# First mixer of a diffusion trunk: scores from plain rows of two heads side by side plus rotary rows in four row groups

## The chip, the cores and the metric

The kernel runs on one NeuronCore of a Trainium2 chip, in one launch. The metric is the time of an execution in device microseconds; several executions give a median. The core has five engines that work beside each other, each in its own program order: TensorE (PE in the profile; its weight loads are PEld), VectorE (DVE), ScalarE (ACT), GpSimd (POOL) and SyncE (SP). Here POOL and SP issue DMAs, and ACT issues a few.

## The reference, cut to what matters

Two groups of tokens, 256 latent and 128 context ones, go through a trunk of two layers. Each layer is a half-step SwiGLU FFN, a mixer and another half-step FFN, all modulated by vectors that come from `SiLU(cond) @ w_mod`. The mixer of layer 0 is multi-head latent attention beside a convolution module:

```
cq, ckv, kr, u = split(h @ w_in, [384, 640, 672])
q = (rms_norm(cq) @ w_qu).reshape(B, S, 8, 64 + 32)       # 64 plain columns, 32 rotary ones, per head
q = concat([q[..., :64], axial_rope(q[..., 64:])])        # latent tokens only
k = concat([k_nope, broadcast(axial_rope(kr))])           # 64 rows of the head, 32 shared by all heads
p = softmax(q @ k.T * 96 ** -0.5); o = p @ v
g = depthwise_conv(a * sigmoid(b), w_dw, 31 taps)         # 512 channels
g = silu(layer_norm(g))
out = concat([o, g]) @ w_out
```

Latent queries read the 128 cached context keys and the 256 latent keys; context queries read the 128 context keys.

## The kernel before, in words

All activations are held turned, channels on the 128 partitions and the 384 tokens (256 latent, then 128 context) along the row. Large products are made of three fp32r products (`mm3`): weights and activations are split into a high part (`hi`, a cast on ACT) and a low part (`lo`, the rest), and `hi*hi + hi*lo + lo*hi` is added up in PSUM. `stream` walks through a list of `Step`s; each has a block of weights that SP loads to `raw`, that is split (`split_hi`, `split_lo`) and that its `mm` then uses. With `add=True` the low part is not made by DVE: ACT writes `-raw` to `lo` and a DMA issued by POOL adds `raw` minus the rounding onto it; in the trace that is an ACTIVATE of L176 and a DMA of L177.

The tile framework decides the order of the instructions on each engine when the kernel is built, from the program order and its own priorities; on the chip each engine follows that order strictly and waits on semaphores.

The first mixer, `mixer_a`, goes through these stages:

1. Seven input units (`in_unit`) of `w_in_a`, in the order `ORD`. Their results start the convolution: for each of four channel blocks 31 taps on DVE (`acc<-ub,vec,acc`, L926 and L929), 124 in all. The taps are put in a background list, and `pop_bg` hands out 9 after each step and after each pair of heads.
2. `p_kr` turns the shared rotary key `krf` and copies its 32 rows (held four times over the 128 partitions) to the upper or lower half of all eight `kT` tiles (L890). A `kT` tile of a head then has 64 plain rows and 64 rows with the rotary part twice.
3. `q_step(0)`, `kv_step`, `q_step(1)`. A query step makes four heads of 128 columns: 64 plain ones, 32 rotary ones and the same 32 with swapped neighbours. DVE multiplies the PSUM result by a table of 1, cos and sin (`ropeaq`, L940); as the key has its rotary rows twice, the product with 128 rows gives the rotated score. `kv_step` makes keys and values, and calls `first`: scores and softmax of the first pair of heads.
4. `rest`: for each of the four pairs, scores of the next pair (`scores`, L674), then transposes, `p @ v` and the softmax of the next pair. A pair's scores fill four PSUM banks of the pool `ps_mm`, which has four. `softmax` takes maxima on DVE (`mx`, L689) and exponentials on ACT (L694). What a pair gives is `t<-ps_ax,g` on DVE (L731), and then split to `MXh`, `MXl`.
5. After the last tap, `conv_ln`: `centre` (PE, L1009, needs all four `acc`), squares, `scale`, `finish`, which gives blocks 4 to 7 of `MXh`, `MXl`.
6. The output projection. The first halves of three steps (72 products, blocks 0 to 3) can run before `conv_ln` is done; the rest (120 products) begins with block 4, and then the next FFN follows.

The second mixer, `mixer_c`, uses the same `attention` with 64-row heads, two of them side by side in the two halves of the array (`pairs`).

## Time and profile before

| | us |
|---|---|
| median of three executions | 1458.6 (1457.44 to 1465.83) |
| the profiled execution's own time | 1458.97 |
| its span, first to last instruction | 1457.1 |
| PE busy in the span | 1429.5 (98%) |
| DVE busy | 1154.0 (79%) |
| ACT busy | 667.9 (46%) |
| first mixer, from its first product to the first product of the next FFN | 302 to 464 on the trace's clock |

The profile gives times of one execution in us from the span's start. In a timeline row the first number is the start, the second how long it lasted, then the engine, the line, the operation and `out<-in`, how many instructions were merged (x), and in square brackets how long the engine had been idle and what ended that. The f32 products of L674 are two instructions each in the trace. Matmuls are pipelined, so that a row of PE lasts longer than the distance to the next start; the distance is what a product costs.

### The profile page before, as it was taken

The page shows a single profiled execution, that of the slowest core. Times are in us where ns is not written, and L with a number is a line of the kernel's source. Part 1 is how long each engine was busy: PE and PEld are TensorE (multiplying, and loading weights), DVE is VectorE, ACT ScalarE, POOL GpSimd, SP SyncE. Part 2 cuts the span into 40 slices and gives each one's busy share as a digit, 9 for nine tenths or more (in the row PEclk, how much of TensorE's full clock was granted, in tenths as well). Part 3 has the DMA queues.
Part 4 walks back from the last instruction along what each step waited for, and adds up shares of the span by engine and source line. Part 5 has one row for each costly group of instructions (what it writes and reads, how often), then busy time and mean ns, then how long its engine had stood idle before and what let it go on. Part 6 is the DMA issues. An engine that isn't in the chain of part 4 may idle for free. (4 is left out here: it accounts for less than half of the span.)

```text
span 1457.1 us, 22136 instructions
## 1 busy us (share of the span) xinstructions
PE 1429.5 (98%) x8450; PEld 1389.4 (95%) x8450; DVE 1154.0 (79%) x2411; ACT 667.9 (46%) x1177; POOL 26.2 (2%) x38
## 2 busy tenths in 40 slices
PE   8999999999999999999999999999998999999997
PEld 6999999999888999999999999999976999999997
DVE  5899999959987999999879996545887698555443
ACT  4534333368766443343343433334477444434332
POOL 0000000021100000000000000000000000000000
PEclk9999999999999999999999999999999999999999
DMA  9666657699656566556565662344310264332341
GB/s 382 253 226 211 234 187 257 238 245 212 150 145 217 188 228 234 206 213 238 199 243 205 232 229 98 104 136 163 130 59 30 86 230 147 137 124 90 118 135 48
DMA packets 45066, 262.55 MB, mean 180 GB/s; under 512 B 4992, under 2 KB 6816, under 8 KB 22048
## 3 DMA queue, kind: packets, MB, share of 16 engines
q1 hardware_dynamic: 38592, 245.04, 46.8%
q0 software_dynamic: 4032, 14.16, 5.2%
q10 hardware_dynamic: 2336, 1.94, 0.4%
q8 instruction: 67, 1.10, 0.3%
q14 instruction: 39, 0.32, 0.1%
HBM read 244.98 MB, written 1.98 MB: 169 GB/s over the span
## 5 line engine op out<-in xcount | busy, mean ns | idle before, releaser
L167 ACT CAST whi<-raw 128x1024 fp32r<-128x1024 f32 (+1 forms) x346 | 328.0, 948 | 569.3 <-PE ps_mm L271 499.0
L269 PE MATMUL ps_mm<-Hh,wlo 128*128 128x386 f32 x1568 | 531.8, 339 | 1.0 <-DMA wlo<-raw 1.0
L270 PE MATMUL ps_mm<-Hl,whi 128*128 128x386 f32 x1568 | 529.8, 338 | 0.0
L271 PE MATMUL ps_mm<-Hh,whi 128*128 128x386 f32 x1568 | 529.3, 338 | 0.0
L179 DVE TENSOR_TENSOR wlo<-raw,whi 128x1024 fp32r<-128x1024 f32 (+2 forms) x318 | 345.8, 1087 | 149.4 <-ACT whi L167 147.3
L269 PEld LDWEIGHTS ps_mm<-Hh,wlo 128*128 128x128 f32 x1568 | 296.2, 189 | 3.2 <-PE ps_mm L271 1.3
L270 PEld LDWEIGHTS ps_mm<-Hl,whi 128*128 128x128 f32 x1568 | 296.3, 189 | 0.5
L271 PEld LDWEIGHTS ps_mm<-Hh,whi 128*128 128x128 f32 x1568 | 296.6, 189 | 0.0
L269 PE MATMUL ps_mm<-Gh,wlo 128*128 128x384 f32 x704 | 236.5, 336 | 0.0
L270 PE MATMUL ps_mm<-Gl,whi 128*128 128x384 f32 x704 | 236.5, 336 | 0.0
L271 PE MATMUL ps_mm<-Gh,whi 128*128 128x384 f32 x704 | 236.5, 336 | 0.0
L387 DVE SCALAR_TENSOR_TENSOR junk<-rawm,eb 128x1024 bf16<-128x1024 f32 x128 | 155.7, 1217 | 1.1 <-ACT eb L148 1.1
L387 DVE SCALAR_TENSOR_TENSOR rawm<-rawm,eb 128x1024 f32<-128x1024 f32 x128 | 155.7, 1216 | 0.3
L269 PEld LDWEIGHTS ps_mm<-Gh,wlo 128*128 128x128 f32 x704 | 132.4, 188 | 0.0
L270 PEld LDWEIGHTS ps_mm<-Gl,whi 128*128 128x128 f32 x704 | 132.4, 188 | 0.0
L271 PEld LDWEIGHTS ps_mm<-Gh,whi 128*128 128x128 f32 x704 | 132.3, 188 | 0.0
L640 ACT CAST Gh<-g 128x384 fp32r<-128x384 f32 x88 | 45.0, 512 | 89.9 <-DVE g L556 89.7
L549 ACT ACTIVATE sa<-ta,ba 128x256 f32<-128x256 f32 (+1 forms) x176 | 70.3, 447 | 4.4 <-DVE ta L546 4.2
L929 DVE SCALAR_TENSOR_TENSOR acc<-ub,vec,acc 128x399 f32<-128x399 f32 x120 | 69.8, 627 | 0.3
L556 DVE SCALAR_TENSOR_TENSOR g<-t,bb,sa 128x256 f32<-128x256 f32 (+1 forms) x176 | 65.2, 411 | 0.3 <-ACT sa L549 0.3
L494 DVE SCALAR_TENSOR_TENSOR X<-ps_mm,mod,X 128x256 f32<-128x256 f32 x88 | 32.7, 411 | 38.6 <-PE ps_mm L271 38.6
L641 DVE TENSOR_TENSOR Gl<-g,Gh 128x384 fp32r<-128x384 f32 x88 | 48.7, 554 | 12.3 <-ACT Gh L640 12.2
(277 smaller groups left out, 1283.2 us busy)
## 6 DMA issues: line engine op xcount, KB each, us to landing
raw<-wi SPq DMA_DIRECT2D x85, 1024.0 KB, 4.8
rawm<-wmt SPq DMA_DIRECT2D x64, 1024.0 KB, 4.9
raw<-wo SPq DMA_DIRECT2D x64, 704.0 KB, 4.1
wlo<-raw POOLq DMA_DIRECT2D x24, 512.0 KB, 6.5
raw<-wia SPq DMA_DIRECT2D x7, 1024.0 KB, 7.9
raw<-wic SPq DMA_DIRECT2D x6, 1024.0 KB, 4.8
raw<-wm SPq DMA_DIRECT2D x5, 1024.0 KB, 13.8
raw<-woc SPq DMA_DIRECT2D x4, 1024.0 KB, 4.8
```

Source lines behind the costliest of these rows:

```text
L167: self.nc.scalar.copy(hi, s.raw[:, c0:c1])
L179: self.nc.vector.tensor_tensor(out=lo, in0=raw, in1=hi.bitcast(F32), op=ALU.subtract)
L269: mm(out, lhsT=lo, rhs=rh, start=start, stop=False)
L270: mm(out, lhsT=hi, rhs=rl, start=False, stop=False)
L271: mm(out, lhsT=hi, rhs=rh, start=False, stop=stop)
L387: self.nc.vector.scalar_tensor_tensor(out=junk, in0=raw[:, i], scalar=1.0, in1=self.eb[:, c], op0=ALU.mult, op1=ALU.mult, accum_out=out[:, ...
L494: nc.vector.scalar_tensor_tensor(out=self.X[:, d, s0:s1], in0=ps[:, s0:s1], scalar=gate[:, d, c:c + 1], in1=self.X[:, d, s0:s1], op0=ALU.m ...
L549: nc.scalar.activation(sa[:, s0:s1], ta[:, s0:s1], AF.Silu, bias=ba[:, c:c + 1])
L556: nc.vector.scalar_tensor_tensor(out=g[:, s0:s1], in0=t2[:, s0:s1], scalar=bb[:, c:c + 1], in1=sa[:, s0:s1], op0=ALU.add, op1=ALU.mult)
L640: self.nc.scalar.copy(hi, src)
L641: self.nc.vector.tensor_tensor(out=lo, in0=src, in1=hi.bitcast(F32), op=ALU.subtract)
L929: nc.vector.scalar_tensor_tensor(out=acc[j], in0=src(t), scalar=w(t), in1=acc[j], op0=ALU.mult, op1=ALU.add)
```

## The change

The 64 plain rows and the 32 rotary rows of a head are treated apart.

- **Query projection.** The weights are unchanged, and hold the swapped columns still. A new `split_sorted` picks from `raw` the 64 plain columns and the 32 rotary ones of the four heads and leaves the swapped ones out. A query step then has three blocks of 128 columns instead of four: the rotary rows of four heads (j = 2, made first), and two blocks with the plain rows of two heads each. The sorted low part is made by DVE, not with `add`.
- **Rotation.** The rotary block is copied to SBUF by ACT, turned by `rope` on DVE (a shuffle, two multiplications, an addition, over 256 columns), and copied by ACT to both halves of a `qR` tile for each pair. The plain blocks go to `qT` by an ACT copy. `ropeaq` and L940 are gone.
- **Keys.** A `kT` tile holds two heads (64 rows each), copied by one ACT instruction. `krf` is kept, with its four copies of the rotary key, and is used directly: the copies of L890 are gone.
- **Scores.** For a pair: the products of the plain rows (64 rows, two heads in two halves of the array) for both blocks of latent queries, then their rotary rows (32 rows; two heads times two blocks in four row groups), added in PSUM; then the same for the context queries. All of this is under `manual_schedule` for PE, so that PE keeps this order.

```
+            for to, of in move:
+                self.nc.scalar.copy(to(hi), of(s.raw))
+            for to, of in move:
+                self.nc.vector.tensor_tensor(out=to(lo), in0=of(s.raw), in1=to(hi).bitcast(F32), op=ALU.subtract)
...
-    def attention(self, heads, pairs, pool=None):
+    def attention(self, heads, pool=None, turned=None):
...
-            for dst, c0, cols, q0 in ((0, 0, slice(0, T), 0), (0, T, slice(T, 512), TL), (1, 0, slice(0, T), P)):
-                for h in hs:
-                    qT, kT, rows = heads[h][:3]
-                    kw = {"tile_position": (rows.start, 0)} if pairs else {}
...
+            def product(h, dst, c0, cols, q0, extra=False):
+                qT, kT, rows = heads[h][:3]
+                if extra:
+                    g = 64 * dst + 32 * heads[h][7]
+                    qT, kT, rows = turned[0][heads[h][6]], turned[1], slice(g, g + 32)
+                nc.tensor.matmul(S[h][dst][:, c0:c0 + cols.stop - cols.start], lhsT=qT[rows, q0:q0 + P],
+                                 rhs=kT[rows, cols], start=not extra, stop=bool(extra) or not turned,
+                                 tile_position=(rows.start, 0))
+
+            q0, q1, qp = (0, 0, slice(0, T), 0), (1, 0, slice(0, T), P), (0, T, slice(T, 512), TL)
+            with self.tc.manual_schedule(engines={mybir.EngineType.PE}) if turned else nullcontext():
+                for parts in ((q0, q1), (qp,)) if turned else ((q0,), (qp,), (q1,)):
+                    for extra in range(1 + bool(turned)):
+                        for part in parts:
+                            for h in hs:
+                                product(h, *part, extra)
...
-                    for h in range(8):
-                        r = slice(64, P) if h % 2 == 0 else slice(0, 64)
-                        nc.scalar.copy(kT[h][r, :], krf[r, :])
...
-                        for h in range(4):
-                            p = (self.ps_tr if u else self.ps_mm)()
+                        for j in (2, 0, 1):
+                            p = get()
                             for k in range(3):
...
-                            nc.vector.tensor_tensor(out=qT[4 * u + h], in0=p[:, :T], in1=ropeq[:, h % 2], op=ALU.mult)
-
-                    return Step(a["wqu"][u], 1536, True, mm, add=True)
+                            if j < 2:
+                                nc.scalar.copy(qT[2 * u + j], p[:, :T])
+                                continue
+                            x = self.tb("t2")
+                            nc.scalar.copy(x, p[:, :T])
+                            self.rope(x[:, :TL], rope[:, 0], rope[:, 1], SWAP8, x[:, :TL], pp)
+                            for i in range(2):
+                                for o in (0, 64):
+                                    nc.scalar.copy(qR[2 * u + i][o:o + 64], x[64 * i:64 * i + 64])
+
+                    return Step(a["wqu"][u], 1536, True, mm, sort=q_sort)
...
-                            nc.scalar.copy(kT[2 * pr][0:64, :], p[0:64, :])
-                            nc.scalar.copy(kT[2 * pr + 1][64:P, :], p[64:P, :])
+                            nc.scalar.copy(kT[pr], p)
```

The order of the instructions moves on all engines, between the first mixer's input units and its output projection, and nowhere else. Two places follow. The first is DVE around the last pair of heads. The `acc` rows are taps, the `mx` rows the softmax maxima, and `t_...<-ps_ax` what a pair gives. Before, from the first maximum of the last pair on:

```order
L689 TENSOR_REDUCE mx<-ps_mm 128x1 x3
L691 TENSOR_TENSOR mx<-mx,nrs 128x2
L689 TENSOR_REDUCE mx<-ps_mm 128x1 x2
L689 TENSOR_REDUCE mx<-ps_mm 128x1
L691 TENSOR_TENSOR mx<-mx,nrs 128x1
L929 SCALAR_TENSOR_TENSOR acc_3048<-ub_3044,vec,acc_3048 128x399
L731 TENSOR_TENSOR t_4233<-ps_ax,g 128x384
L929 SCALAR_TENSOR_TENSOR acc_3047<-ub_3043,vec,acc_3047 128x399
L641 TENSOR_TENSOR MXl<-t_4233,MXh 128x384
L696 RECIPROCAL sm<-sm 128x6
L929 SCALAR_TENSOR_TENSOR acc_3048<-ub_3044,vec,acc_3048 128x399 x4
L731 TENSOR_TENSOR t_4305<-ps_ax,g 128x384
```

(Rows that only repeat are left out: in all, 10 taps stand between that maximum and `t_4305`, and 6 more between `t_4305` and the first row of `conv_ln`.) Now:

```order
L718 TENSOR_REDUCE mx<-ps_mm 128x1 x5
L720 TENSOR_TENSOR mx<-mx,nrs 128x2
L718 TENSOR_REDUCE mx<-ps_mm 128x1
L720 TENSOR_TENSOR mx<-mx,nrs 128x1 x2
L953 SCALAR_TENSOR_TENSOR acc_3045<-ub_3041,vec,acc_3045 128x399 x4
L760 TENSOR_TENSOR t_4253<-ps_ax,g 128x384
L953 SCALAR_TENSOR_TENSOR acc_3045<-ub_3041,vec,acc_3045 128x399
L657 TENSOR_TENSOR MXl<-t_4253,MXh 128x384
L725 RECIPROCAL sm<-sm 128x6
L760 TENSOR_TENSOR t_4325<-ps_ax,g 128x384
L431 TENSOR_TENSOR Hl<-mod_6_2722,Hh 128x2 x8
L657 TENSOR_TENSOR MXl<-t_4325,MXh 128x384
```

Of the 124 taps, 16 stood behind the last pair's first maximum; now 5 do, and 11 have moved ahead of it.

The second place is PE at the scores of the second pair (`kT_3034` and `kT_3035` before; `kT_3033` and `qR_3029` now). The `ps_tr<-whi,cath` rows are the values of `kv_step`, the `ps_tr<-cqh` rows `q_step(1)`. Before:

```order
L674 MATMUL ps_mm<-kT_3034,qT_3026 128x384
L674 MATMUL ps_mm<-kT_3034,qT_3026 128x128
L712 MATMUL ps_ax<-cst,Hh 128x128
L674 MATMUL ps_mm<-kT_3035,qT_3027 128x384
L674 MATMUL ps_mm<-kT_3035,qT_3027 128x128
L674 MATMUL ps_mm<-kT_3034,qT_3026 128x384
L674 MATMUL ps_mm<-kT_3035,qT_3027 128x384
L269 MATMUL ps_tr<-whi,catl 128x512
```

Now, with 12 products of `kv_step` and the 27 of `q_step(1)` between the first row and the later ones:

```order
L694 MATMUL ps_mm<-kT_3033,qT_3025 128x384 x4
L285 MATMUL ps_tr<-whi,catl 128x512
L287 MATMUL ps_tr<-cqh,whi 128x384
L694 MATMUL ps_mm<-krf,qR_3029 128x384 x4
L694 MATMUL ps_mm<-kT_3033,qT_3025 128x128 x2
L694 MATMUL ps_mm<-krf,qR_3029 128x128 x2
L741 MATMUL ps_tr<-cst,Hh 128x128 x4
```

The whole pair was scored ahead of `q_step(1)`; now its plain rows are, and its rotary rows and context queries follow behind it.

In the output projection PE now has 48 of the 72 first-half products behind the last product of `centre`; before it had 37.

43 lines of the change are left out of this document (29 added, 14 removed).

## The prediction

> **What bounds the kernel now.** I read the page's totals, then the busy time by stages of the first mixer, then who waits for whom there, then its last stretch instruction by instruction.
>
> ```profile
> PE 1429.5 (98%) x8450; PEld 1389.4 (95%) x8450; DVE 1154.0 (79%) x2411; ACT 667.9 (46%) x1177; POOL 26.2 (2%) x38
> ```
>
> PE is busy nearly always, so a product less should be time less, unless PE waits in the stage that the change touches. The stages (columns: length, then busy time of PE, PEld, DVE, ACT and POOL with instruction counts, PE's granted clock, DMA share, GB/s):
>
> ```profile
> 348.00:380.00 32.00, 29.98 (x161) 27.88 (x160) 29.15 (x71) 24.39 (x40) 6.91 (x8) 1.00 0.92 215
> 380.00:392.00 12.00, 12.00 (x55) 9.25 (x54) 11.24 (x27) 8.90 (x20) 0.79 (x1) 1.00 0.06 22
> 392.00:402.00 10.00, 10.00 (x73) 8.81 (x72) 9.63 (x25) 10.00 (x23) 1.27 (x3) 1.00 0.83 184
> 402.00:412.00 10.00, 10.00 (x67) 7.15 (x67) 9.58 (x25) 8.16 (x21) 1.38 (x2) 1.00 0.94 227
> 430.00:442.00 12.00, 8.64 (x51) 7.90 (x50) 7.51 (x29) 9.03 (x14) 1.72 (x2) 0.96 0.77 210
> 442.00:464.00 22.00, 22.00 (x121) 22.00 (x120) 15.83 (x38) 14.19 (x28) 0.86 (x1) 0.94 0.49 132
> ```
>
> From 348 to 412 DVE is busy 59.60 of 64 us: its idle time is 2.85 + 0.76 + 0.37 + 0.42 = 4.4 us. PE looks just as full, but from 430 to 442 it stands still for 3.4 us. The waits name the cause:
>
> ```profile
> PE ps_mm L269 <- ACT MXh L640: 3.2, 1, 3.2
> PE ps_mm L269 <- DMA wlo<-raw: 2.0, 2, 1.0
> ...
> DVE mx L689 <- PE ps_mm L674: 2.2, 2, 1.8
> DVE acc L1013 <- PE ps_ax L1009: 1.9, 1, 1.9
> ```
>
> PE's longest wait in the mixer is for `MXh` of the convolution's layer norm. In the timeline:
>
> ```profile
> 420.51 1.68 PE L728 MATMUL ps_ax<-Hl,Vt 128*64 128x256 f32 x16
> 422.37 0.55 DVE L731 TENSOR_TENSOR t<-ps_ax,g 128x384 f32<-128x384 f32 x1
> ...
> 426.05 1.30 DVE L929 SCALAR_TENSOR_TENSOR acc<-ub,vec,acc 128x399 f32<-128x399 f32 x2
> 427.74 1.48 PE L1009 MATMUL ps_ax<-acc,cst 128*128 128x256 f32 x10
> 429.26 1.68 DVE L1013 SCALAR_TENSOR_TENSOR acc<-ps_ax,acc 128x256 f32<-128x256 f32 x6 [1.91 <-PE ps_ax L1009]
> 437.34 0.54 PE L473 MATMUL ps_ax<-cst,r 128*128 128x128 f32 x3 [0.18 <-DVE r L489]
> 441.06 1.61 PE L269 MATMUL ps_mm<-MXh,wlo 128*128 128x384 f32 x4 [3.18 <-ACT MXh L640]
> ```
>
> The last pair's `p @ v` ends at 422.2, the last tap at 427.35, `centre` at 429.2, and PE starts again at 441.06. So the mixer's end is set by **DVE's taps** and the chain behind them, not by PE's products. A product less on PE makes the wait at 441 longer, not the kernel shorter.
>
> That wait costs more than its 3.18 us:
>
> ```profile
> 443.11 0.53 PE L270 MATMUL ps_mm<-MXl,whi 128*128 128x384 f32 x1
> 443.43 0.53 PE L271 MATMUL ps_mm<-MXh,whi 128*128 128x384 f32 x1
> ...
> 444.64 0.33 PE L269 MATMUL ps_mm<-MXh,wlo 128*128 128x384 f32 x1
> 444.81 0.34 PE L270 MATMUL ps_mm<-MXl,whi 128*128 128x384 f32 x1
> ```
>
> Behind it products start 0.32 us apart, from 444.64 on 0.17 to 0.18. From 441.06 to 444.64, 11 products took 3.58 us instead of 11 × 0.175 = 1.93: **1.65 us** lost, and the stage's clock is 0.94.
>
> **The change part by part.**
>
> *PE, query projection.* Two steps of 36 products become two of 27: 18 fewer.
>
> ```profile
> 365.79 0.34 PE L270 MATMUL ps_mm<-cql,whi 128*128 128x384 f32 x1
> 365.96 0.34 PE L271 MATMUL ps_mm<-cqh,whi 128*128 128x384 f32 x1
> ```
>
> At 0.175 us from start to start that is 18 × 0.175 = 3.2 us. Nine of them (1.6 us) lie ahead of a wait that they only lengthen:
>
> ```profile
> 366.14 0.86 POOL L177 DMA_DIRECT2D wlo<-raw  x1 [2.03 <-ACT wlo L176]
> 374.07 0.50 PE L269 MATMUL ps_mm<-cath,wlo 128*128 128x512 f32 x1 [1.03 <-DMA wlo<-raw]
> ...
> wlo<-raw POOLq DMA_DIRECT2D x24, 512.0 KB, 6.5
> ```
>
> `kv_step`'s second low part is issued at 366.14 and lands at 374.07; its issue does not depend on the query products. The four low-part DMAs of the query weights go away, which may let it land sooner, by 1.4 us if it took the 6.5 us that such DMAs take in the median (the last row). So the first pair's scores start where they did, at best 1.4 us earlier.
>
> *PE, scores.* A pair before, and two 64-row heads side by side, as the second mixer shows them:
>
> ```profile
> 379.05 3.19 PE L674 MATMUL ps_mm<-kT,qT 128*128 128x384 f32 x12
> 381.78 0.69 PE L270 MATMUL ps_tr<-wlo,cath 128*128 128x512 f32 x1
> ...
> 1093.53 1.78 PE L674 MATMUL ps_mm<-kT,qT 64*128 64x384 f32 x12
> 1095.25 0.33 PE L712 MATMUL ps_tr<-cst,pr 128*128 128x128 f32 x1
> ```
>
> Before: 2.73 us for 1792 columns. The plain rows now: 1.72. The rotary rows are in no trace. If four (then two) run wholly side by side they cost 2.73 × (384 + 128) / 1792 = 0.78; if they run one by one, 2.73. A pair then takes 2.50 to 4.45 us. I take 2.7, near the lower end, since the 64-row products do run side by side: no gain, no loss.
>
> [...]
>
> *DVE, new work.* Nearest rows (columns: count, busy us, mean ns; and, in the second fence, the key's rotation and nine taps in a row):
>
> ```profile
> L929 DVE SCALAR_TENSOR_TENSOR acc<-ub,vec,acc 128x399 f32<-128x399 f32 x84 | 48.6, 625 | 0.1
> L641 DVE TENSOR_TENSOR MXl<-t,MXh 128x384 fp32r<-128x384 f32 x4 | 2.2, 550 | 0.0
> L940 DVE TENSOR_TENSOR qT<-ps_tr,ropeaq 128x384 f32<-128x384 f32 x4 | 2.2, 556 | 0.4 <-PE ps_tr L271 0.2
> L940 DVE TENSOR_TENSOR qT<-ps_mm,ropeaq 128x384 f32<-128x384 f32 x4 | 2.1, 546 | 0.0
> ```
> ```profile
> 339.81 0.45 DVE L647 STREAM_SHUFFLE rp<-krf 128x256 f32<-128x256 f32 x1
> 341.23 0.42 DVE L649 TENSOR_TENSOR krf<-krf,ropea 128x256 f32<-128x256 f32 x1
> ...
> 373.02 4.98 DVE L929 SCALAR_TENSOR_TENSOR acc<-ub,vec,acc 128x399 f32<-128x399 f32 x9
> ```
>
> Gone: 8 multiplications, 4.3 us. New: two rotations of a shuffle and three operations, 2 × (0.45 + 3 × 0.42) = 3.4; four subtractions of 384 columns, 4 × 0.55 = 2.2; four of 192 columns, in no trace, between half of that and all of it each (0.28 to 0.55), I take 0.35: 1.4. That is 7.0 - 4.3 = 2.7 busy, between 2.4 and 3.5. Neighbours overlap by some 0.08 us (the nine taps took 4.98 us, 0.55 each, against a mean of 0.625), and there are eight more of them: **2.0 us**.
>
> *DVE, moved work.* As the change shows, 11 taps moved ahead of the last pair's first maximum: 11 × 0.55 = **6.0 us** in a queue that takes its instructions in order. The first maxima of the first and the last pair were at:
>
> ```profile
> 380.76 1.22 DVE L689 TENSOR_REDUCE mx<-ps_mm 128x1 f32<-128x384 f32 x3 [1.82 <-PE ps_mm L674]
> 412.08 1.21 DVE L689 TENSOR_REDUCE mx<-ps_mm 128x1 f32<-128x384 f32 x3
> ```
>
> The last one had no wait: DVE came late by its own work. It is now due at 412.08 + 6.0 + 2.0, less what of the 4.4 us of idle time is filled. All could be, or none; I take 2.0, about what DVE's two waits for scores (2.2) make up. That gives 418.1, 6.0 us later (3.6 to 8.0).
>
> *ACT.* It loses the eight copies of `krf` and half of the key copies, ahead of 380; it gains 14 short copies, seven of them around 392 to 402, where it is busy 10.00 of 10.00. I cost this at nothing, since DVE is later by more; without that cover it is 7 × 0.5 = 3.5 us on the exponentials.
>
> *From there to the end.* The last `p @ v` ended 10.1 us behind the last pair's first maximum; nothing in that chain changes, so 428.2 now. `centre` no longer finds taps in front of it, but follows after `t`, `MXh` and `MXl` of the pair (three operations of some 0.55 us with their hand-over, 2.0), six products (1.05) and its own rows (14 instructions now, 2.0 by 1.48 for 10): 433.2, **4.0 us later** than 429.2. Behind it 48 filler products stand instead of 37, 11 × 0.175 = 1.9 us, which first fill PE's time until L473 and push that back by up to 1.9 us; some is won back, as the activation table's load and two splits on ACT no longer stand between, so I count **0.5 us**. PE's wait for the convolution's `MXh` is then some 2 us instead of 3.18, too short for the slow stretch by this trace's one case: **-1.65**.
>
> Sum: 4.0 + 0.5 - 1.65 = +2.85. On the profiled execution's 1458.97 (span 1457.1) that is 1461.8; its time was 0.4 above the median of 1458.6, so I predict **1461.4 us**, 0.2% slower, no change by measure.
>
> [...]
>
> **The rivals.**
>
> - *PE's gain arrives.* DVE's idle time takes up the new work, and the last maximum moves by under 3.6 us. For it: PE is 98% busy, and 4.4 us of idle time are there. Against: 8.0 us have to fit in. Then `centre` is no later than before, PE arrives 3.2 us earlier at a wait of the same end, and only the slow stretch can go: 1459.0 - 1.65 = 1457.3; if `centre` even gets 3 us earlier, 1454. Chance 0.24.
> - *Slower, at the third pair's scores.* A pair needs four banks. Before, its first four products used only the first two; now the third product needs the third bank, so that PE stands until the pair before has done all six exponentials. Two of these stand behind a cast of `MXh` on ACT, which waits for a `t` that now stands behind six maxima and five taps on DVE. If PE stands there for over some 3 us, it also falls to half speed: 1.65 us more, and 2 us later scores. It decides once scores come later than DVE reaches the maximum. 1461.4 + 3.7 = 1465. Chance 0.18.
> - *The four row groups don't run side by side.* Then a pair takes 4.45 us, 1.72 more. Where DVE waits for scores (two pairs in the trace) it counts: +3.5, up to +7 for all four: 1465 to 1468. Chance 0.10.
> - The forecast, 1459 to 1464: chance 0.48.
>
> **How the numbers follow.** The range from 1455.5 to 1466.5 leaves out the lower half of the first rival (0.1) and the upper parts of the other two (0.1); it holds the bounds of the last maximum (3.6 to 8.0 against 6.0, so 1459 to 1463.4). A measurement of this kernel can't tell less than 1%, 14.6 us, from no change, and no case reaches that: within 1% 0.97, faster 0.01, slower 0.02.
>
> **What would show it.** Right: the last pair's first maximum near 418, `centre` done near 433, PE's wait for `MXh` shorter than 3.18 us and no products 0.32 us apart behind it; `kv_step`'s wait for `wlo` longer than before; a pair's scores in 2.5 to 3 us. Wrong: `centre` before 429, or a pair's scores over 4 us, or a granted clock under 1 between 380 and 430.

## The result and the profile after

| | before | after |
|---|---|---|
| median of six executions each, us | 1458.99 (1457.44 to 1465.83) | 1473.2 (1470.19 to 1476.76) |
| the profiled execution's own time, us | 1458.97 | 1476.76 |
| its span, us | 1457.1 | 1475.0 |
| ratio of the times, 95% interval | | 1.0082 (1.0061 to 1.0102) |

The change made the kernel slower by 0.8%, some 12 us (the two medians lie 14.2 us apart). That is less than the 1% that was set as the bound of "no change", but it lies outside the predicted range (1455.5 to 1466.5), and the interval excludes both no difference and the forecast of +2.4 us. So a difference under 1% can be told here, which the prediction had doubted. The profiled execution is the slowest of its six. A second profile of the same kernel (e12, 1469.82 us) is used below wherever it matters which of the differences come back.

The totals (the same row as before), and the busy time by stages of the first mixer (columns as in the prediction):

```profile
PE 1442.3 (98%) x8480; PEld 1393.2 (94%) x8480; DVE 1158.1 (79%) x2421; ACT 665.4 (45%) x1179; POOL 22.8 (2%) x34
```
```profile
392.00:402.00 10.00, 5.34 (x40) 3.94 (x39) 9.40 (x25) 7.52 (x14) 1.72 (x2) 0.86 0.93 195
402.00:412.00 10.00, 10.00 (x59) 5.84 (x58) 5.05 (x11) 6.51 (x18) 0.86 (x1) 0.80 0.29 100
412.00:430.00 18.00, 16.57 (x122) 10.70 (x121) 16.20 (x41) 11.96 (x35) 0.00 (x0) 0.91 0.31 88
442.00:464.00 22.00, 18.99 (x105) 18.71 (x105) 12.01 (x40) 15.82 (x25) 2.59 (x3) 0.92 0.71 169
```

PE is busy for 12.8 us more with 30 instructions more, DVE and ACT for about as long as before. From 392 to 402 PE was busy for 10.00 of 10 us before. Now it stands still for 4.7 of these 10 us, and its clock falls to 0.86, then 0.80, in a part of the mixer that had run at 1.00. And DVE, which had been busy for 9.58 of 10 us from 402 to 412, has half of that stretch free (5.05). The waits between 340 and 480 say the same from both sides:

```profile
DVE t L760 <- PE ps_ax L757: 10.3, 3, 5.4
...
PE ps_tr L745 <- ACT Hl L743: 4.7, 1, 4.7
```

DVE now waits 10.3 us for `p @ v` of the pairs; PE waits 4.7 us in one place for ACT. One large cause stands at about 400. ACT and PE there (timeline):

```profile
395.63 2.09 ACT L987 COPY qR<-t 64x384 f32<-64x384 f32 x4
400.16 1.04 ACT L183 CAST whi<-raw 128x1024 fp32r<-128x1024 f32 x1 [2.45 <-DMA raw<-woa]
401.12 0.58 ACT L743 COPY Hl<-ps_tr 128x512 f32<-128x512 f32 x1
```
```profile
396.82 0.27 PE L741 MATMUL ps_ax<-cst,Hh 128*128 128x128 f32 x1
401.75 0.90 PE L745 MATMUL ps_tr<-cst,Hh 128*128 128x128 f32 x3 [4.66 <-ACT Hl L743]
```

ACT's queue holds, behind its four copies of turned rows, a cast of a weight of the output projection. The weight's DMA has not landed, ACT stands for 2.45 us and then casts for 1.04, and behind that stand the copies of the first pair's transposes, for which PE waits 4.66 us. PE's first product of the output projection comes at 427.75, so nothing needs the weight yet.

How the loss grows over the pairs is read from DVE's first maximum of each pair (before: 380.76, 392.08, 402.91, 412.08):

```profile
379.60 0.56 DVE L718 TENSOR_REDUCE mx<-ps_mm 128x1 f32<-128x384 f32 x1
...
396.25 2.14 DVE L718 TENSOR_REDUCE mx<-ps_mm 128x1 f32<-128x384 f32 x5
...
412.31 0.56 DVE L718 TENSOR_REDUCE mx<-ps_mm 128x1 f32<-128x384 f32 x1
...
423.87 2.14 DVE L718 TENSOR_REDUCE mx<-ps_mm 128x1 f32<-128x384 f32 x5
```

and from the end of the mixer, DVE's rows and PE's:

```profile
434.26 0.56 DVE L760 TENSOR_TENSOR t<-ps_ax,g 128x384 f32<-128x384 f32 x1 [3.32 <-PE ps_ax L757]
...
439.38 1.68 DVE L1060 SCALAR_TENSOR_TENSOR acc<-ps_ax,acc 128x256 f32<-128x256 f32 x6 [3.42 <-PE ps_ax L1056]
```
```profile
452.47 0.97 PE L285 MATMUL ps_mm<-MXh,wlo 128*128 128x384 f32 x4 [3.01 <-ACT MXh L656]
...
454.18 0.52 PE L285 MATMUL ps_mm<-MXh,wlo 128*128 128x384 f32 x1
454.50 0.52 PE L286 MATMUL ps_mm<-MXl,whi 128*128 128x384 f32 x1
```

PE's restart behind the convolution's `MXh` moves from 441.06 to 452.47, by 11.4 us. Below, "restart" is this row, and the kernels on whose steps the argument rests are laid out by the five steps that lead to it. Each row is one execution: that of e2 is the fastest of twelve (4.0 us below its median), those of e17 and e14 the slowest of eight and of six (6.0 and 5.2 above), and that of e8 the fastest of six (8.1 below).

| kernel (profiled) | first pair's first maximum | 1st to 2nd pair | 2nd to 3rd | 3rd to 4th | 4th pair's maximum to restart | restart |
|---|---|---|---|---|---|---|
| before | 380.76 | 11.32 | 10.83 | 9.17 | 28.98 | 441.06 |
| after | 379.60 | 16.65 | 16.06 | 11.56 | 28.60 | 452.47 |
| e12, after again | 379.65 | 16.64 | 16.76 | 9.94 | 28.60 | 451.59 |
| e4, projection alone | 380.87 | 15.11 | 11.28 | 8.78 | 28.53 | 444.57 |
| e6, e4 with DVE relieved | 381.42 | 12.26 | 10.40 | 8.43 | 28.55 | 441.06 |
| e3, no rotary products | 382.13 | 14.51 | 10.79 | 9.19 | 28.57 | 445.19 |
| e1, after without the wait for the weight | 379.45 | 16.67 | 13.50 | 9.97 | 31.83 | 451.42 |
| e2, order of scores as before | 379.72 | 15.29 | 10.52 | 10.25 | 30.89 | 446.67 |
| e9, e2 with both edits on GpSimd | 382.25 | 16.50 | 15.80 | 10.04 | 31.24 | 455.83 |
| e13, e9 without the wait for the weight | 383.27 | 18.00 | 12.30 | 11.69 | 31.33 | 456.59 |
| e11, e9 with PE's order fixed | 382.29 | 18.06 | 16.10 | 10.04 | 31.24 | 457.73 |
| e10, after with both edits on GpSimd | 383.68 | 18.99 | 17.20 | 10.21 | 28.52 | 458.60 |
| e14, e10 without the wait for the weight | 385.87 | 19.59 | 13.49 | 12.03 | 28.66 | 459.64 |
| e8, e1 with the copies on GpSimd | 380.61 | 17.14 | 13.49 | 10.87 | 29.90 | 452.01 |
| e17, e2 with one of them (split) | 383.90 | 16.62 | 10.05 | 10.03 | 31.22 | 451.82 |
| e18, e2 with the other (copies) | 382.31 | 15.24 | 16.00 | 9.77 | 31.14 | 454.46 |

Of the 11.41 us, 5.33 come between the first and the second pair, 5.23 between the second and the third, and 2.39 between the third and the fourth; 1.16 are won ahead of them and 0.38 behind. In e12 the steps lie within 1.7 us of these. Who sets the pace differs between these steps (columns as above):

```profile
380.76:392.08 11.32, 11.32 (x51) 8.72 (x50) 11.32 (x27) 8.24 (x19) 0.86 (x1) 1.00 0.03 9
```
```profile
379.60:396.25 16.65, 16.41 (x82) 11.74 (x81) 16.41 (x40) 13.06 (x27) 1.92 (x3) 1.00 0.27 51
396.25:412.31 16.06, 11.40 (x69) 7.00 (x68) 10.70 (x27) 9.79 (x23) 1.53 (x2) 0.79 0.57 148
```

The first row is the step from the first to the second pair before, the other two are the first two steps after. In the first step DVE is full, before and after: 23 taps stand in it instead of 16, which is where most of the moved taps went, and the second pair's scores too are ready only at 395.7. Between the second and the third pair **DVE no longer sets the pace**: it is busy for 10.70 of 16.06 us.

The span behind the restart is 1016.0 us before and 1022.5 after; in e12 it is 1016.4. So the 6 us that the profiled execution loses there belong to that execution (the last section), not to the change.

### The profile page after: what moved, and what is told of

Same layout as the page of the kernel before. It is cut to its first block, busy times and chain, and to the rows that moved or that the text cites. A ratio compares the mean times of both kernels' runs of the same rounds, so it can differ in the third digit from the quotient of the medians.

```text
span 1475.0 us, 22188 instructions
## 1 busy us (share of the span) xinstructions
PE 1442.3 (98%) x8480; PEld 1393.2 (94%) x8480; DVE 1158.1 (79%) x2421; ACT 665.4 (45%) x1179; POOL 22.8 (2%) x34
```

## The experiments

Each kernel was compared with the kernel before on the same chip; ratios are to that, with 95% intervals. The theories: the long scores with their rotary products; A, ACT's wait for the output weight; VectorE's new work in the projection; D, ACT's new load; G, the order of the scores' products. The three first runs took the change apart on the side of the scores.

**e1: the cast and the split of that weight on GpSimd**, so that nothing on ACT waits for its DMA.

```
-        self.nc.scalar.copy(hi, s.raw[:, c0:c1])
+        self.nc.gpsimd.tensor_copy(hi, s.raw[:, c0:c1])     # shortened: for this one half of a step alone
...
+        self.nc.gpsimd.tensor_tensor(out=lo, in0=raw, in1=hi.bitcast(F32), op=ALU.subtract)
```

> The changed kernel, with one edit: the cast and the subtraction that split the fourth half of the output weights (woa) are done by GpSimd instead of ScalarE and a DMA, so that ScalarE's queue no longer holds a cast that waits for these weights ahead of the first pair's copies of Hl. Theory A (the wait): the loss is PE's 4.66 us at 401.75 and the half clock behind it, 4.15 us long, which costs 2.1; without the cast PE's wait there falls under 2.5 us and the kernel takes 1465 to 1468. Theory B (the products): the loss is the scores' own PE time, 17.9 us for four pairs instead of 11.7; then the time stays at 1471 to 1474, as what PE doesn't lose there it loses at the end of the mixer.

Measured: 1469.43 us, ratio 1.0055 (1.0034 to 1.0077). The wait of 4.66 us at 401.75 has shrunk to one of 1.26 at 398.23, but there is a shorter one at each of the two pairs that follow (PE's timeline, and the stretch behind the second of these waits):

```profile
406.06 0.91 PE L700 MATMUL ps_mm<-kT,qT 64*128 64x384 f32 x2 [1.84 <-ACT Hl L729]
...
413.49 0.91 PE L700 MATMUL ps_mm<-kT,qT 64*128 64x384 f32 x2 [1.44 <-ACT Hh L729]
```
```profile
415.50:425.60 10.10, 10.10 (x49) 6.60 (x50) 9.02 (x22) 4.44 (x13) 0.00 (x0) 0.50 0.00 0
```

These are the first plain products of the third and the fourth pair, which wait for a bank until the pair before has done its exponentials, as the second rival had it for the third pair. By the table, 2.56 us are won between the second and third pair and 1.59 behind it, and 3.2 are given back at the end. Of these, 2.7 come ahead of the last pair's `t` (432.69 in e1, 434.26 in the change), where PE now runs for 10.2 us, from 415.4 to 425.7, at half its clock, the last pair's scores included; in the profile after that was 3.4 us. So the half clock moved with the waits. The edit has a price of its own too: while GpSimd splits the weight, DVE's taps take twice as long (five taps each, after, then e1, and GpSimd's work in e1):

```profile
398.79 2.81 DVE L953 SCALAR_TENSOR_TENSOR acc<-ub,vec,acc 128x399 f32<-128x399 f32 x5
```
```profile
398.65 5.68 DVE L959 SCALAR_TENSOR_TENSOR acc<-ub,vec,acc 128x399 f32<-128x399 f32 x5
```
```profile
400.11 1.16 POOL L185 CAST whi<-raw 128x1024 fp32r<-128x1024 f32 x1 [3.33 <-DMA raw<-woa]
401.35 2.55 POOL L196 TENSOR_TENSOR wlo<-raw,whi 128x1024 fp32r<-128x1024 f32 x1
```

DVE, which waits in this step of the change, has no wait in it here (busy for 13.50 of 13.50 us), and 2.9 us of that are these taps' excess. In e8 and e14 five taps take 5.67 us beside the same work, and in e13 a DVE row of 128x1, at 405.37, takes 2.32 us. So e1 does not price the wait for the weight by itself, and neither does any kernel below that moves this split to GpSimd. The restart comes 1.05 us earlier in the trace (0.2 against e12); the ratio is 0.27% lower, some 4 us, with intervals that overlap. So the wait for the weight is a part of the loss; that it isn't the larger one is likely and not shown.

**e2: the scores' products in the order of before** (first block of queries, context, second block; each with its rotary rows), not fixed by hand.

```
-            with self.tc.manual_schedule(engines={mybir.EngineType.PE}) if turned else nullcontext():
-                for parts in ((q0, q1), (qp,)) if turned else ((q0,), (qp,), (q1,)):
+            with nullcontext():
+                for parts in ((q0,), (qp,), (q1,)):
```

> The changed kernel, with the scores' products in the order of before (first block of both heads, context block, second block, each plain product followed by its rotary one) and no fixed order on PE. ScalarE's queue then has an exponential ahead of the first pair's copies of Hl and the cast of the woa weights behind them. Theory A (the wait): no wait for Hl over 2 us, 1465 to 1468. Theory B (the products): the same 96 products stay, with two more changes of row groups for each pair; a pair takes 4 us or more and the time stays at 1471 to 1475.

Measured: 1467.39 us, ratio 1.0041 (1.0029 to 1.0054), the best version of the whole change. Two things differ: a pair asks for its banks two at a time, and ACT's cast comes at 404.01, where the DMA has landed. The step from the second to the third pair is as long as before (10.52). One pair's scores, undisturbed:

```profile
412.02 0.92 PE L694 MATMUL ps_mm<-kT,qT 64*128 64x384 f32 x4
412.87 0.91 PE L694 MATMUL ps_mm<-krf,qR 32*128 32x384 f32 x4
413.71 0.49 PE L694 MATMUL ps_mm<-kT,qT 64*128 64x128 f32 x4
414.14 0.49 PE L694 MATMUL ps_mm<-krf,qR 32*128 32x128 f32 x4
414.56 0.92 PE L694 MATMUL ps_mm<-kT,qT 64*128 64x384 f32 x4
415.40 0.91 PE L694 MATMUL ps_mm<-krf,qR 32*128 32x384 f32 x4
```

In this execution PE's clock is 1.00 throughout the mixer. From start to start each group (the products that run side by side) of 384 columns costs 0.84 to 0.85 and each of 128 columns 0.42 to 0.43: 4 x 0.85 + 2 x 0.42 = 4.2 us a pair, against 2.73 before. What is left of the loss stands between the first and second pair (15.29) and at the end (30.89). DVE is busy for 35.23 of the 36.06 us of the three steps between the pairs, with 21, 11 and 12 taps in them instead of 16, 9 and 9: without ACT's wait it sets the pace again, longer scores or not.

**e3: the change without the rotary products.** The output lacks the rotary part of the scores.

```
-                    for extra in range(1 + bool(turned)):
+                    for extra in range(1):
```

> The changed kernel without the 32-row rotary products (the scores lack the rotary part; all copies, rotations and splits for it stay). Theory B (the products): the rotary products cost PE 0.85 + 0.42 us a pair, and without them the plain ones run as in the second mixer, 1.7 to 2.4 a pair; PE gets 5 to 9 us back and the kernel takes 1459 to 1466. Theory A (the wait): the scores' PE time is hidden, and as long as ScalarE waits for the woa weights ahead of the copies of Hl the time stays above 1468; ScalarE's queue has this cast elsewhere here, so the trace has to say whether it waits.

Measured: 1461.75 us, ratio 1.0006 (0.9991 to 1.0021). The rotary products and what follows from them cost 0.8%: the order of the instructions changes with them, and ACT has no wait for the weight here. In the trace the restart is at 445.19, beside e4's 444.57: without them the scores cost nothing, and the rest of the lateness is the projection's. By the ratio hardly any lateness is left; the two readings differ by some 3 us.

**e4: the projection alone.** Queries and keys are put together again to tiles of 128 rows (64 plain, 32 rotary, 32 zeros), and the scores are those of before.

```
+                            for o in (0, 64):
+                                nc.scalar.copy(qT[4 * u + 2 * j + o // 64][o:o + 64], p[o:o + 64, :T])
...
+                            for i in range(4):
+                                nc.scalar.copy(qT[4 * u + i][o:o + 32], x[32 * i:32 * i + 32])
```

> Only the query projection of the change: sorted weights, 18 products fewer, rotation of the rotary rows on DVE, short copies on ScalarE; the scores are made as before from 128 rows of one head (64 plain, 32 rotary, 32 of zeros). Theories A and B both put the loss into the scores and their order: 1456 to 1460, as before or up to 3 us faster. Rival C: the loss is in the projection's new work on DVE and ScalarE (my own forecast had 4 us later centre from it): 1462 to 1466.

Measured: 1465.55 us, ratio 1.0027 (1.0012 to 1.0042): slower by 3.9 us by the ratio (5.2 by the medians) though PE has 18 products less. The last pair's maximum, `centre` and the restart:

```profile
416.04 1.21 DVE L718 TENSOR_REDUCE mx<-ps_mm 128x1 f32<-128x384 f32 x3
...
433.15 2.21 DVE L1066 SCALAR_TENSOR_TENSOR acc<-ps_ax,acc 128x256 f32<-128x256 f32 x8 [1.68 <-PE ps_ax L1062]
```
```profile
431.60 1.51 PE L1062 MATMUL ps_ax<-acc,cst 128*128 128x256 f32 x10
444.57 0.97 PE L285 MATMUL ps_mm<-MXh,wlo 128*128 128x384 f32 x4 [2.66 <-ACT MXh L656]
```

`centre` ends at 433.1. Of the lateness, 3.79 us come between the first and second pair, where the second query step's split and rotation stand on DVE; it is busy there for 13.76 of 15.11 us, and 1.35 go to two waits for ACT. The taps have hardly moved: 18, 9 and 9 stand between the pairs and 16 behind the last maximum, where the kernel before has 16, 9, 9 and 16.

**e5 and e6: e4 with the short copies on GpSimd (e5), then with the low part's subtractions there too (e6).**

```
-                                nc.scalar.copy(qT[4 * u + i][o:o + 32], x[32 * i:32 * i + 32])
+                                nc.gpsimd.tensor_copy(qT[4 * u + i][o:o + 32], x[32 * i:32 * i + 32])
...
-                self.nc.vector.tensor_tensor(out=to(lo), in0=of(s.raw), in1=to(hi).bitcast(F32), op=ALU.subtract)
+                self.nc.gpsimd.tensor_tensor(out=to(lo), in0=of(s.raw), in1=to(hi).bitcast(F32), op=ALU.subtract)
```

> The kernel with the projection alone (scores from 128 rows as before), and its eight short copies of rotary rows (32 rows of 384 columns, 0.52 us each) on GpSimd instead of ScalarE. Theory D (ScalarE's queue): in the second query step ScalarE has no pause from 383.6 to 400.8, and PE waits 2.28 us at 397.63 for a bank that ScalarE empties behind 2.07 us of short copies; with these gone PE's wait there is under 0.8 us and the kernel takes 1461 to 1463.5. Theory E (VectorE): the loss of the projection is VectorE's new work (two rotations, eight subtractions for eight multiplications); then the time stays at 1464.5 to 1467. A rival to both: GpSimd's copies take far longer than 0.52 us and the rotary rows come late to the third and fourth pairs' scores.

> As the run with the short copies on GpSimd, and the eight subtractions that make the low parts of the sorted query weights on GpSimd as well instead of VectorE (3.6 us of VectorE in all). Theory D (ScalarE's queue): within 1 us of the run with the short copies alone. Theory E (VectorE): 2 to 3.5 us less than that run. Rival: the subtraction is slow on GpSimd (no trace shows it), PE waits longer for the first low part than the 1.24 us at 356.81 and the time is 1 to 4 us higher.

Measured: e5 1464.18 us, 1.0014 (0.9997 to 1.0031); e6 1461.67 us, 0.9996 (0.998 to 1.0011). e5 takes 2.0 of the 2.28 us of a wait for ACT away from PE (at 397.6), but its first maximum comes 3.3 us later (384.20 against 380.87), and its restart is at 445.66, no earlier than e4's. In e6 every mark of the mixer's end is back where it was before:

```profile
412.51 1.22 DVE L718 TENSOR_REDUCE mx<-ps_mm 128x1 f32<-128x384 f32 x3
```
```profile
427.98 1.48 PE L1062 MATMUL ps_ax<-acc,cst 128*128 128x256 f32 x10
441.06 1.65 PE L285 MATMUL ps_mm<-MXh,wlo 128*128 128x384 f32 x4 [3.01 <-ACT MXh L656]
```

Against e5, only the subtractions have left DVE, and that gives 4.6 us at the restart and 2.5 by the medians (the intervals overlap; those of e4 and e6 don't). So the projection's loss is DVE's new work, the subtractions above all, and the 3 us that PE is spared bring nothing even then, because PE meets the same wait at the same time. The subtractions on GpSimd without the copies were not tried on the projection alone.

**e7: the kernel before, with seven of the short copies added on ACT.**

```
+                                    nc.scalar.copy(junk[o:o + 64], qT[4 * u + h][o:o + 64])   # shortened: seven, in the second query step
```

> The kernel before, unchanged but for seven short copies on ScalarE (64 rows of 384 columns, 0.5 us each, into a tile that nobody reads) behind the multiplications of the second query step. Theory D (ScalarE's queue): 3.5 us more on ScalarE where it is full delay the exponentials and Hl of the first pairs, so the kernel gets 2 to 4 us slower: 1462 to 1465. Theory E (VectorE): ScalarE has room there, 1459.5 to 1461.5 as before.

Measured: 1462.12 us, ratio 0.9997 (0.9981 to 1.0013), restart at 441.64. ACT's load by itself costs nothing, so theory D falls as a matter of load; these copies release no bank and nobody reads them, so a copy that stands in the way of PE is not tested by it.

**e8 to e11, e13, e14: the whole change with the relief of e6.** e8 is e1 with the copies of `qR` on GpSimd. e9 and e10 are e2 and the change with both edits of e6 (copies and subtractions on GpSimd); e11 is e9 with PE's order fixed by hand. e13 and e14 are e9 and e10 with e1's edit as well.

```
-                                    nc.scalar.copy(qR[2 * u + i][o:o + 64], x[64 * i:64 * i + 64])
+                                    nc.gpsimd.tensor_copy(qR[2 * u + i][o:o + 64], x[64 * i:64 * i + 64])
```

> The changed kernel with the fourth half of woa split on GpSimd (as in the first experiment) and the eight short copies of rotary rows (64 rows) on GpSimd too. Theory D (ScalarE's queue): PE's wait for Hl at 398 (1.26 us in the first experiment) goes and the kernel takes 1465 to 1467.5; what then is left over the kernel before, 5 to 7 us, is the scores' own PE time (theory B). If ScalarE's queue were not the cause, the time would stay at 1469.

> The change with its projection's short copies and low-part subtractions on GpSimd (which made the projection alone cost nothing) and the scores' products in the order of before, no fixed order on PE. What is left over the kernel before is the scores' own cost. Theory B (the products): 19 us of PE for four pairs instead of 11.7, of which the end of the mixer sees what lies behind the last pair's maxima and in front of them: 2 to 4 us over before, 1462 to 1466. Rival F (all hidden): PE waits at the mixer's end anyway, so the scores cost nothing: within 1 us of before.

> The same relief on GpSimd with the changed kernel's own order of products, fixed on PE (both blocks of both heads, their rotary products in four row groups, then the context blocks). Theory G (the order): the third product of a pair needs the third bank, so PE stands until the pair before has done its exponentials; waits of 1 to 3 us stand ahead of pairs three and four, and the kernel is 3 to 7 us slower than the one with the order of before: 1467 to 1471. If the order is harmless and only ScalarE's wait for the woa weights counted: within 1.5 us of it, if no such wait is in the trace.

> The same relief, the order of before (each block's plain products followed by its rotary ones), but fixed on PE within a pair. Against the run that leaves this order open it shows what the fixing costs. Theory G (the order of the products): as that run within 1.5 us. Rival H (the fixing itself): as slow as the run with the change's own order, 1467 to 1471.

> The kernel of the run with relief and the order of before (1475.5), with the fourth half of the woa weights split on GpSimd, so that ScalarE doesn't hold a cast that waited 4.40 us for these weights ahead of the second pair's exponentials. Theory A (that wait is the loss): no wait of ScalarE for a DMA in the trace, and 1463 to 1467, 8 to 12 us faster. Theory B (the products alone): the scores' 19 to 21 us of PE are still there; 1472 to 1475.

> The same without that wait, in the changed kernel's own order of products, fixed on PE. Theory G (the order costs by itself, as the third product of a pair needs the third bank): 2 to 5 us slower than the run with the order of before and no wait, with PE waits of 1 to 3 us at the first plain products of pairs three and four. Theory A alone: within 1.5 us of that run.

| | median, us | ratio (95%) |
|---|---|---|
| e8 | 1477.93 | 1.0096 (1.0073 to 1.0119) |
| e9 | 1475.53 | 1.0100 (1.0083 to 1.0117) |
| e10 | 1476.27 | 1.0109 (1.009 to 1.0127) |
| e11 | 1476.57 | 1.0109 (1.009 to 1.0128) |
| e13 | 1476.15 | 1.0104 (1.008 to 1.0127) |
| e14 | 1476.47 | 1.0106 (1.0085 to 1.0128) |

e8, e9, e10 and e13 missed; e11 and e14 came within 1.5 us of e9 and e13, as one of their two cases had it. What healed the projection made the whole change as slow as it had been, or slower, whatever the order of the products (e9 against e10, e13 against e14) and whether or not it was fixed (e9 against e11). So theory G, that the order by itself costs, has no support in the times; in the traces the restart comes 2.8 and 3.05 us later with the change's order, and that stays open. Taking the wait for the weight away (e13 against e9) won 3.5 us between the second and third pair, by the table, and lost 1.0, 1.5 and 1.65 in the steps around it. Here too waits and half clock moved: in e9 to e11, e13 and e14 PE waits 1.9 to 3.3 us for the first pair's exponentials at the second pair's scores, and its clock is 0.50 for 3.4 to 10.2 us from 386 to 388 on, where the change has none of this. It lies in their first step, which takes 16.5 to 19.6 us (15.29 in e2), and it hides what the other edits are worth. e8's timed executions lay some 8 us above its profiled one (1469.88); their mean granted clock was 0.987 to 0.991, and 0.995 in the profiled one, which points to more time at half clock; where is not on record.

**e12: the change once more, profiled only.**

> The changed kernel as it is, once more, for a second profile: which of its losses come back. The 4.66 us wait for Hl at 401.75 and the waits ahead of pairs three and four are in the program's order and should come back within 1 us. The half clock in the second mixer at 1088 (3.2 us lost, behind a wait of 1.18 us that the kernel before has too without loss) should come and go with the executions. The next stage's products 177.8 ns apart instead of 175 (2.8 us): no theory; back if it lies in the program, gone if in the execution.

1469.82 us. The wait for the weight (ACT 2.40, PE 4.61 us) comes back, and so do the steps of the table.

**e15 and e16: ten taps of the convolution on GpSimd**, in the kernel before (e15) and in e6 (e16), to see what shorter DVE queues bring.

```
+                            nc.gpsimd.tensor_scalar(out=to, in0=src(t), scalar1=w(t), scalar2=None, op0=ALU.mult)
...
+                                nc.gpsimd.tensor_tensor(out=part, in0=part, in1=prod, op=ALU.add)
...
+                        fs.append(lambda: nc.vector.tensor_tensor(out=acc[0], in0=acc[0], in1=part, op=ALU.add))
```

> The kernel before, with ten of the 124 taps (the last ten of the first channel block) made by GpSimd as a product and a sum each, and added by one VectorE operation; VectorE has nine operations of 0.55 us less, 5 us. If VectorE's queue sets the end of the mixer, as the prediction read it: centre is up to 5 us earlier and PE's wait for MXh shorter; 1456 to 1460 against 1461 to 1462 for before. If PE sets it: no change. Rival: GpSimd's 19 operations hold up its DMA issues for the low parts; slower.

> The projection of the change with its copies and subtractions on GpSimd and 128-row scores (as fast as before), and the same ten taps on GpSimd. If VectorE's queue sets the end: with 18 products fewer on PE and nine operations fewer on VectorE it gains more than the kernel before does from the taps alone, 1454 to 1458. If PE's 3.2 us are hidden by something else: as the kernel before with fewer taps, within 1 us.

Measured: 1475.76 us, 1.0099 (1.008 to 1.0119), and 1477.05 us, 1.0108 (1.0086 to 1.013). Both miss, since GpSimd pays more than DVE would (e15, groups by line; busy us, mean ns):

```profile
L936 POOL TENSOR_SCALAR prod<-ub,vec 128x399 f32<-128x399 f32 x9 | 13.8, 1537 | 0.5
L938 POOL TENSOR_TENSOR part<-part,prod 128x399 f32<-128x399 f32 x9 | 10.4, 1155 | 0.6
```

A tap costs 2.7 us there, against 0.55 on DVE, and the DMAs that GpSimd has to issue for the low parts stand behind them: the first scores start at 391.38 instead of 379.05. PE's clock is 0.50 there for 13.7 us between 340 and 361, which is in that lateness too. From there to the restart e15 takes 60.65 us, and before 62.01: 1.4 us is all that ten taps fewer on DVE brought within the pairs, so these two do not settle how much DVE's queue is worth.

**e17 and e18: the two edits of e9 one at a time**, on e2: subtractions on GpSimd (e17), copies of `qR` on GpSimd (e18). The diffs are those of e6 and e8.

> The kernel of e2, with one edit: the eight low parts of the sorted query weights are subtracted on GpSimd. The short copies of the turned rows stay on ScalarE. Of the two edits that together took e2 from 1467.4 to 1475.5 (e9), this does the first alone. Theory one (e9's loss is the first pair's late rotary rows, four GpSimd copies of 0.8 us each instead of ScalarE's 0.5): then this kernel gains what VectorE is relieved of, as e6 did against e4, 2 to 4 us: 1464 to 1466, and the first pair's first maximum comes near 380.7. Theory two (the loss hangs on the subtractions, which move the rest of ScalarE's queue, with the cast of woa ahead of a pair's exponentials): 1473 to 1476, and ScalarE waits for woa over 2 us in the trace.

> The kernel of e2, with one edit: the eight short copies of the turned query rows are made by GpSimd instead of ScalarE. The subtractions stay on VectorE. Theory one (e9's loss is the first pair's late rotary rows): 1473 to 1476, the first pair's first maximum near 383.5. Theory two (the loss hangs on the subtractions): 1466 to 1469, as e2.

Measured: e17 1467.91 us, 1.0053 (1.0032 to 1.0074); e18 1473.28 us, 1.0083 (1.0057 to 1.011). By these times the copies are what makes e9 slow; the subtractions bring nothing and cost little. In e18 (GpSimd, ACT and PE):

```profile
376.10 3.14 POOL L987 COPY qR<-t 64x384 f32<-64x384 f32 x4 [8.29 <-issue]
```
```profile
402.61 1.04 ACT L183 CAST whi<-raw 128x1024 fp32r<-128x1024 f32 x1 [4.36 <-DMA raw<-woa]
```
```profile
404.85 0.90 PE L745 MATMUL ps_tr<-cst,Hh 128*128 128x128 f32 x3 [4.42 <-ACT Hl L743]
```

The four copies take 3.14 us on GpSimd and 2.09 on ACT, and the first maximum comes 2.6 us later than in e2 (382.31 against 379.72). With ACT's copies gone, the cast is reached earlier than its DMA, as in the change itself, and 5.5 us are lost between the second and third pair. Over all kernels of the table that step takes 15.8 to 17.2 us with ACT's wait for the weight, and 10.05 to 13.5 without. In e17 the first scores come 2.3 us later (377.55 against 375.27 in e2), which is likely why the gain on DVE doesn't arrive. Why they do is open: ACT's first cast of the sorted weights is as late already (354.06 against 351.74), before GpSimd splits any of them. Its profile, the slowest of eight, also has 6.8 us at half clock from 382.5 on, so that the table's row for it shows both.

## Why the prediction was wrong

The sign was right and the size was not: +2.4 us said, some 12 measured. Two of the signs of being wrong that the prediction named came about: a pair's scores took over 4 us, and the granted clock fell below 1 between 380 and 430.

- **What bounds the kernel: right for the projection, not kept up for the scores.** That DVE's chain sets the end and PE's spared products bring nothing is shown by e4 and e6. The step that failed was to go on with DVE as the pace of all pairs. Between the second and the third pair DVE waits for 5.4 us in all; such a step is paced by the round scores, maximum, exponentials, transposes, `p @ v`, and a stop of ACT or a longer product delays it. It was ACT's stop that took the pace from DVE: in e2, with scores longer still and no such stop, DVE is full again.
- **PE, query projection: the gain right, the wait wrong.** The 54 products take 9.74 us, 3.0 less than the 72 before (3.2 said). The wait for `wlo` in `kv_step` was to be longer; it is gone. Its DMA was issued at 365.23 instead of 366.14, with the four low-part DMAs of the query weights out of its way, and the first scores start at 375.15, 3.9 us earlier (at best 1.4 said). Only 1.16 of that reached the first maximum, because a pair's first score is complete only when its rotary rows are added.
- **PE, scores, "I take 2.7 ... no gain, no loss": the step that failed most.** The first pair after the change:

```profile
375.15 1.55 PE L694 MATMUL ps_mm<-kT,qT 64*128 64x384 f32 x6
377.09 0.91 PE L694 MATMUL ps_mm<-kT,qT 64*128 64x384 f32 x2 [0.38 <-ACT kT L999]
377.93 0.93 PE L694 MATMUL ps_mm<-krf,qR 32*128 32x384 f32 x8
378.78 0.49 PE L694 MATMUL ps_mm<-kT,qT 64*128 64x128 f32 x4
379.20 0.49 PE L694 MATMUL ps_mm<-krf,qR 32*128 32x128 f32 x4
379.62 0.50 PE L285 MATMUL ps_tr<-whi,catl 128*128 128x512 f32 x1
```

  That is 4.47 us with a wait of 0.38. The four row groups do run side by side (0.85 for four products of 384 columns, as much as two take), so the mechanism of the third rival falls, though a pair takes nearly the 4.45 us that it gave. But a group of 384 columns that stands between other row groups costs 0.85 and one of 128 columns 0.42, with 64 rows as with 32. By my shares, 0.78 us stood for the rotary rows, and they took 0.85 + 0.42 = 1.27; 1.72 stood for the plain rows, and they took 2.4 and 0.42. The four pairs took 4.1, 5.1, 4.7 and 4.0 us, 17.9 in all against 11.7 before, and I had kept the upper bound of 4.45 only for the case that nothing ran side by side. The price of a short group (0.42 for 128 columns, where a third of 0.85 would be 0.28) gives, as an estimate from these two prices, a fixed cost of some 0.2 us per change of row groups by (3 x 0.42 - 0.85) / 2, and 0.645 and 0.215 us for the columns. The second mixer's pair, whose groups follow one another without a change, bears it out: 2 x 0.645 + 0.215 + 0.205 = 1.71, and it takes 1.72. In the change's order a pair then takes, by the same estimate, 3.2 us (0.205 + 2 x 0.645, 0.85, and twice 0.42); the rest, 0.8 to 0.9 in the first and the fourth pair, is one plain product that runs apart from the other, since it waits for `kT` or a bank.
- **DVE, new and moved work: right for the new work, half right for the moved taps.** In the change the last maximum is at 423.87, not at 418.1; the chain from there to `centre` takes 15.5 us (15.1 said). Of the 11 moved taps 7 went into the first step, where DVE is full and they count; in the next step DVE waits for others anyway. In e4 the last maximum is 3.96 us later and `centre` ends at 433.1, which looks like the forecast (3.6 to 8.0 later, 433.2), but by luck: in e4 no taps moved, and `centre` follows the last maximum by 17.1 us as before. By e6 its 3.5 us at the restart are DVE's.
- **ACT, "I cost this at nothing": failed, by a cause that it did not look at.** The load costs nothing (e7, ratio 0.9997). What costs is that ACT's order has a cast of a weight, whose DMA is late, ahead of copies for which PE waits: 4.66 us of PE's time, and half the clock from 399.1 to 405.9, that is for 4.2 us behind the wait. e1 gave back some 4 us of the 12 by the ratios (1.05 at the restart), e2 some 6 by both, the latter together with the order of the scores.
- **The slow stretch, "-1.65": failed.** It was to go since the wait would be some 2 us. The wait is 3.01 us, and products stand 0.32 us apart behind it again; in e4 the wait was 2.66 us, and its products stand 0.32 us apart from 445.91 on. No run shows a length of wait that decides it, neither these 2 us nor the second rival's 3: behind 1.27 us it was 0.50 in the profile after and 1.00 in e12, and behind 3.01 us in e2 the products start 0.17 to 0.18 us apart.
- **The second rival** had the step (from the second to the third pair) and half the mechanism: waits of PE for exponentials are there, in the change at the fourth pair (1.27 us at 414.33) and in e1 at the third and the fourth (1.84 and 1.44), but the larger one is ACT's wait for a DMA, and the price was 5.2 us in that step instead of 3.7 in all.

Taken together: of some 12 us, about 4 are DVE's work for the projection (e4, e6), and about 8 come with the rotary products (7.3 at the restart by e3 against the change, 7.9 by e4; by e3's ratio 11). Of these 8, some 4 to 6 went with ACT's wait or the order of the scores (e1, e2); what is left are longer scores and the taps that moved with them. How these divide is open, since taking the wait away alone gave some 4 us in the change and nothing in e9, each time at the price of slower taps, and since PE's half clock moved to another place each time; no run holds that clock fixed. No version that was run is faster than the kernel before; e6, without the new scores, equals it.

## What to carry to other kernels

A product's price is its own duration in the form in which it will run, and a group of few columns or few rows is not the share of its multiplications (here 0.42 us for 128 columns beside 0.85 for 384, and 0.85 for 32 rows as for 64): measure it, or take the upper bound as the forecast. When an engine's share of a loop grows, ask again, step by step, what paces the loop, since the slack of the others was measured under the old pace. And in an in-order queue an instruction that waits for a DMA is the whole queue's wait (here 2.45 us on ACT, and 4.66 on PE behind it): look for weight casts that a new order puts ahead of what the critical loop needs. Before a step's length is put down to an edit, look at the granted clock in that step, in both traces (here 0.50 in some stretches, 1.00 in most).

## What the runs showed of the hardware

Whether the clock halves does not follow from a wait's length alone. The change twice, at the same wait of 1.27 us, with the clock of the stretch of 3.4 us behind it, first in the profile after:

```profile
414.33 0.91 PE L694 MATMUL ps_mm<-kT,qT 64*128 64x384 f32 x2 [1.27 <-ACT Hh L723]
```
```profile
416.20:419.60 3.40, 3.40 (x22) 2.02 (x18) 2.00 (x4) 3.13 (x11) 0.00 (x0) 0.50 0.73 294
```

and then in e12:

```profile
415.07 0.91 PE L694 MATMUL ps_mm<-kT,qT 64*128 64x384 f32 x2 [1.27 <-ACT Hh L723]
```
```profile
416.20:419.60 3.40, 3.40 (x34) 2.24 (x33) 3.40 (x8) 3.40 (x12) 0.00 (x0) 1.00 0.75 267
```

In the one the granted clock is 0.50, in the other 1.00, so one wait of 1.27 us was enough in the one execution and not in the other. The restart shows the same: a wait of 3.01 us is followed by no time at half speed in e2, by 3.4 us in the profile after, and in e6 by 5.75 us behind the wait. In the profile after the slow stretches begin or end at 399.11, 405.94, 416.18, 419.59, 453.73, 457.14, 1088.60 and 1095.43, all on one grid of 3.413 us (696.32 us from the first to the last, 204 steps). In e17 the clock falls at 382.50 behind waits of only 0.32 and 0.43 us, among products of 64 and 32 rows; why is open. At the second mixer a wait of 1.18 us (1072.60 before, 1086.79 after) was followed by 6.8 us at half speed after and by none before: some 3 us, and since neither e12 nor the kernel before has them, they belong to the execution. A second such difference has no wait at all: from 480 to 660 the profile after holds 1013 products, before 1031 and e12 1030, that is 0.178 us from start to start instead of 0.175, some 3 us, at a granted clock of 1.00. Its cause is open. Together these two make up the 6 us between executions of one kernel, and this is why the steps above are compared within the mixer.

GpSimd beside ACT and DVE: four copies of 64 x 384 in 3.14 us (e18) against 2.09 (after), a tap in 2.7 (e15) against 0.55 (before). And DVE was slower beside its work: beside its cast and subtraction of 128 x 1024, five taps took 5.68 us instead of 2.81 (e1; 5.67 in e8 and e14). Why is open.
